# Summing modulation rows over the partitions: matmuls with a tile of ones, or transfers that accumulate in place

## The chip, the cores and the metric

The kernel runs on one core of a Trainium2 chip. The metric is the device time of one execution in microseconds (us); the median of three runs of the kernel before is 1470.62 us, from 1469.34 to 1471.14. A core has five engines with their own instruction queues, each run in order: TensorE (PE; its weight loads are shown as PEld), VectorE (DVE), ScalarE (ACT), GpSimd (POOL) and SyncE (SP). Here SP issues the loads of weights and the stores of the output, and POOL issues the small transfers of the modulation.

## The reference, cut to what matters

A layer of a diffusion backbone on 256 latent tokens and 256 context tokens of width 2048. A conditioning vector c gives six rows of 2048 numbers, by which the tokens are shifted, scaled and gated:

```python
mod = (jax.nn.silu(c) @ w_mod[l] + b_mod[l])[:, None, :]
sa, ca, ga, sm, cm, gm = jnp.split(mod, 6, axis=-1)
...
mix = token_mixer(q, k_all, v_all, p[..., P_OFF:G_OFF], p[..., G_OFF:], lam, lam_init, ...)
x = x + ga * mix
x = x + gm * sq_relu_mlp(modulate(x, norm_mlp_w[l], sm, cm), w_ff1[l], w_ff2[l])
```

`modulate(x, w, shift, scale)` is `rmsnorm(x, w) * (1 + scale) + shift`. The first two rows, `sa` and `ca`, are needed at the start. The four late ones, `ga`, `cm`, `sm` and `gm`, are needed from the output projection on. Each of them is a product of one vector of 2048 with a 2048 x 2048 matrix, plus a bias.

## The kernel before

All products of the layer are made of 128x512 or 128x256 tiles. A weight chunk of 128x1024 floats is loaded by SP into a `raw` tile (five buffers), ACT casts it to `whi` (L243), DVE subtracts to get the rest `wlo` (L244), three buffers each, and PE multiplies the high and the low part (`xstat`, L453, L454 and L459; `ff1`, L1061 and L1064). PE's instructions follow the order of the program, and so does most of DVE's; the rest is ordered by a scheduler when the kernel is built. The stages are: first modulation rows and the first q and k groups, then v, q, k, v groups, pooling (`pin`), gates (`pg`, `pyy`) beside attention, output projection (`wo`), and the MLP (`f`).

The four late rows are made beside this work, not on PE. `late_gen` (L612) is a generator that is advanced by one step whenever enough weight chunks have passed: a step loads one 128x1024 chunk of the row's matrix, and DVE multiplies it by 128 numbers of silu(c), one for each partition, and adds it to an accumulator (`late_part`, L651, tile `macc`). After 16 such steps the accumulator holds, for half a row (1024 columns), one partial sum in each of 128 partitions. Its start was a memset by POOL and a load of the bias into partition 0 (L632, L633). There are 4 rows of 2 halves.

The partial sums must be added over the partitions, and the sum is wanted in all 128 partitions, because it multiplies tokens, which lie in the partitions. That is done with PE: for each quarter row the 512 columns are split into a high and a low part (`late_half`: cast on ACT, L270, `ah`; subtraction on DVE, L271, `al`), and two matmuls with a 128x128 tile of ones (`late_sum`, L670 and L671) put the sum into every partition of a PSUM bank. ACT copies it to its place (L675), or, for `cm`, DVE adds 1 and multiplies by the norm weights (L673, tile `nmw`, loaded in 128 copies, L640). As `macc` has one buffer, what is left of a half is made up before the next begins (L627 to L630).

Where these steps stand in the queues is set by `later(n, fn)` (L96): it keeps a step back until n more weight chunks have been taken, and `tick` (L100) then writes it out. `pin` keeps an instruction in the written order on its engine.

The readers of the four rows: `ga_bc` in `projected` (L924), `cm` (first part of the tile `sb`) in `scaled` (L918), `sm` (second part of `sb`) in `shifted` (L955), `gm` at the end (L1092, L1104).

Other work on POOL near the change: sums of rotated q and k (`qraw`, L484), limits of squares in attention (`osq`, L754, read by PE's `osum`, L758), window sums of the pooling (`za`, L811 to L818), squares in the MLP (L1041, L1072).

Of the kernel before, what the change touches and what calls it, by code (L numbers as in the profile page):

```python
# [11 lines left out]
F32 = mybir.dt.float32  # L12
F32R = mybir.dt.float32r
AF = mybir.ActivationFunctionType
ALU = mybir.AluOpType
AX = mybir.AxisListType

P = 128
# [30 lines left out]
def layer(ctx: ExitStack, tc, a, out):  # L49
    nc = tc.nc  # L50
    pool = ctx.enter_context(tc.tile_pool(name="sb", bufs=1))
    psum = ctx.enter_context(tc.tile_pool(name="ps", bufs=8, space=bass.MemoryType.PSUM))
    pe, gp = nc.tensor, nc.gpsimd
    pin = tc.keep_in_program_order
    ordered = [False]
# [13 lines left out]
    act, vec, pe, sp = Engine(nc.scalar, ordered), Engine(nc.vector, ordered), Engine(nc.tensor, ordered_pe), nc.sync  # L69

    def bank(name):
        return psum.tile([P, 512], F32, tag="ps", name=name)

    def work(name, shape=None, dt=F32):
        return pool.tile(shape or [P, 512], dt, tag="w2", name=name, bufs=9)
# [14 lines left out]
    late = [None]  # L90
    credit = [0.0]
    credit_rate = [0.0]
# [3 lines left out]
    def later(n, fn):  # L96

        waiting.append([n, fn])
# [170 lines left out]
    def split(hi, lo, src):  # L269
        act.copy(hi, src)  # L270
        vec.tensor_sub(lo, src, hi.bitcast(F32))  # L271
# [33 lines left out]
        return prq[:, lo:hi]  # L305

    ident = pr("ident")
    ones = pool.tile([P, P], F32R, tag="ones", name="ones")
    vec.memset(ones.bitcast(F32), 1.0)
    ebias = pool.tile([P, 1], F32, tag="ebias", name="ebias")  # L310
    vec.memset(ebias, -32.0 * math.log(2.0))
    epsb = pool.tile([P, 1], F32, tag="epsb", name="epsb")
# [294 lines left out]


    ga_bc = s8("ga_bc", [P, D])
    parts = []  # L610

    def late_gen():  # L612
        for name in ("ga", "cm", "sm", "gm"):
            if name == "ga":
                dst = ga_bc
            elif name == "gm":
                mods["gm"] = None
                yield
                mods["gm"] = s8("gm_bc", [P, D])
                dst = mods["gm"]  # L620
            else:
                if "sb" not in mods:
                    mods["sb"] = s16("sb", [P, 2, D])
                dst = mods["sb"][:, 0 if name == "cm" else 1, :]
            for half in range(2):
                yield
                for part in parts:  # L627
                    if part in waiting:
                        waiting.remove(part)
                        part[1]()  # L630
                acc = pool.tile([P, 1024], F32, tag="macc", name="macc", bufs=1)
                gp.memset(acc, 0.0)  # L632
                nc.gpsimd.dma_start(acc[0:1, :], a["b_" + name][half])  # L633
                norm_w = []
                for k in range(KT):
                    raw = raw_chunk(a["w_" + name][half, k])
                    if name == "cm" and k == 8:
                        for q in range(2):
                            norm_w.append(work("nmw"))
                            nc.gpsimd.dma_start(norm_w[q], a["nmw"][2 * half + q])  # L640
                    later(2 if credit_rate[0] < 1 else 1, partial(late_part, acc, raw, k))
                    parts.append(waiting[-1])
                    if k == KT - 1:
                        o = dst[:, half * 1024:half * 1024 + 1024]
                        later(2 if credit_rate[0] < 1 else 1, partial(late_split, acc, norm_w, o))
                        parts.append(waiting[-1])
                    yield

    def late_part(acc, raw, k):

        pin(vec.scalar_tensor_tensor(acc, raw, sil[:, 0, k:k + 1], acc, ALU.mult, ALU.add))  # L651

    def late_split(acc, norm_w, o):
        for q in range(2):
            part = partial(late_half, q, acc, norm_w, o)
            if q == 0:
                part()
            else:
                later(2, part)
                parts.append(waiting[-1])  # L660

    def late_half(q, acc, norm_w, o):
        ah, al = work("ah", dt=F32R), work("al", dt=F32R)
        split(ah, al, acc[:, q * 512:q * 512 + 512])
        later(3, partial(late_sum, ah, al, norm_w[q] if norm_w else None, o[:, q * 512:q * 512 + 512]))

    def late_sum(ah, al, wr, o):

        ps = bank("late")
        pin(pe.matmul(ps, ones, ah, start=True, stop=False))  # L670
        pe.matmul(ps, ones, al, start=False, stop=True)  # L671
        if wr is not None:
            vec.scalar_tensor_tensor(o, ps, 1.0, wr, ALU.add, ALU.mult)  # L673
        else:
            act.copy(o, ps)  # L675

    late[0] = late_gen()

# [449 lines left out]
def _layout(inp):  # L1128
    f = {k: np.asarray(v) for k, v in inp.items()}
    m = {}  # L1130

    def put(name, arr):
        m[name] = np.ascontiguousarray(arr)

    for n, s in (("xT", "x"), ("cT", "ctx")):
        put(n, f[s][0].T.reshape(4, 4, P, T).transpose(0, 2, 1, 3))
    put("x", f["x"][0].reshape(2, P, 4, 512).transpose(0, 2, 1, 3))

    wm, bm = f["w_mod"][0], f["b_mod"][0]
    chunk = {n: slice(i * D, (i + 1) * D) for i, n in enumerate(("sa", "ca", "ga", "sm", "cm", "gm"))}  # L1140
    both = np.stack([wm[:, chunk[n]].reshape(4, 4, P, KT, 128) for n in ("ca", "sa")], 4)
    put("w_m", both.transpose(3, 0, 2, 1, 4, 5).reshape(KT, 4, P, 1024))
    for n in ("ga", "cm", "sm", "gm"):
        put("w_" + n, _ko(wm[:, chunk[n]]))
        put("b_" + n, bm[chunk[n]].reshape(2, 1, 1024))
    put("nmw", np.broadcast_to(f["norm_mlp_w"][0].reshape(4, 1, 512), (4, P, 512)))

    wi = f["w_in"][0]
    put("w_q", _xs(wi[:, 0:1024]))
    put("w_k", _xs(wi[:, 1024:2048]))  # L1150
    put("w_v", _xs(wi[:, 2048:3072]))
    put("w_p", _ws(wi[:, 3072:4096]))
    put("w_ga_in", _xs(wi[:, 4096:6144]))
    put("w_gb_in", _xs(wi[:, 6144:8192]))
    put("pool_w", f["pool_w"][0].reshape(4, 2, P, T).transpose(0, 2, 1, 3).reshape(4, P, 512))
    put("w_a", _xs(f["w_a_up"][0]))
    put("w_b", _xs(f["w_b_up"][0]))
    put("w_o", _xs(f["w_o"][0]))
    put("w_ff1a", _ko(f["w_ff1"][0][:, :1024])[0])
    put("w_ff1", _ws(f["w_ff1"][0][:, 1024:]))  # L1160
    w2 = f["w_ff2"][0].reshape(8, 1024, D)
    put("w_ff2", np.stack([_xs(w2[b]) for b in range(8)]))

    edge = []
    t = np.arange(T)
    for w in WINDOWS:
        cnt = np.clip(t + w // 2, 0, T) - np.clip(t - w // 2, 0, T)
        e = np.float32(w) / cnt.astype(np.float32)
        ee = np.concatenate([e[:w // 2], e[T - (w // 2 - 1):] if w > 2 else e[:0]])
        edge.append(np.concatenate([ee, np.zeros(2 * (w - 1) - len(ee), np.float32)]))  # L1170
    edge = np.concatenate(edge)
    pc = {"ident": np.eye(P, dtype=np.float32), "c": _cols(f["c"][0]), "cc": _cols(f["c_ctx"]),
          "bsa": _cols(bm[chunk["sa"]]), "bca": _cols(bm[chunk["ca"]]), "nw": _cols(f["norm_attn_w"][0]),
          "pscale": _cols(f["pool_scale"][0]), "subln": f["subln_w"][0][:, None],
          "edge": np.broadcast_to(edge, (P, len(edge))), "stack": np.tile(np.eye(32, dtype=np.float32), (4, 1))}
    prm = np.zeros((P, PRM_W), np.float32)
    for n, v in pc.items():
        lo = PRM[n][0]
        prm[:, lo:lo + v.shape[1]] = v
    m["prm"] = prm  # L1180

    inv = (np.float32(10000.0) ** (-np.arange(0, 32, 2, dtype=np.float32) / np.float32(32))).astype(np.float32)
    row = (t // 64).astype(np.float32)[:, None] * inv[None]
    col = (t % 64).astype(np.float32)[:, None] * inv[None]
    cos = np.concatenate([np.cos(row), np.cos(row), np.cos(col), np.cos(col)], 1)
    sin = np.concatenate([-np.sin(row), np.sin(row), -np.sin(col), np.sin(col)], 1)
    pc = {"cos": cos.reshape(2, P, 64).transpose(1, 0, 2).reshape(P, 128),
          "sin": sin.reshape(2, P, 64).transpose(1, 0, 2).reshape(P, 128),
          "wq": f["q_norm_w"], "wk": f["k_norm_w"], "lq1": f["lambda_q1"], "lk1": f["lambda_k1"],
          "lq2": f["lambda_q2"], "lk2": f["lambda_k2"]}  # L1190
    prq = np.zeros((P, PRQ_W), np.float32)
    for n, v in pc.items():
        lo, hi = PRQ[n]
        prq[:, lo:hi] = np.broadcast_to(v, (P, hi - lo))
    m["prq"] = prq
    return m
# [15 lines left out]
```

## Time and profile before

| | us |
|---|---|
| median of three runs | 1470.62 |
| the profiled execution | 1469.82 |
| its span, first to last instruction | 1467.8 |
| busy: PE / DVE / ACT / POOL | 1437.1 / 1000.2 / 683.5 / 121.3 |

How to read rows of the profile. In a timeline a row is: start in us, duration in us, engine, line, operation, tile written <- tiles read, shape, count, and in brackets how long the engine was idle before it and what ended that. Durations of matmuls overlap, so the pitch from start to start says what one costs. A row of a window is: stretch, its length, then for PE, PEld, DVE, ACT and POOL the busy time with the number of instructions, then the granted clock of PE as a share of full speed, the busy share of the DMA engines and GB/s. A row of a tile is: line, engine, operation, tile, count, shortest/median/longest duration in ns, first and last start; the row on landing gives the time from issue to the data's arrival of the transfers named above it.

### The profile page before, as it was taken

To read this page: it belongs to the slowest core of one execution; us is meant where nothing else is said; L and a number is where in the kernel's file an instruction comes from. 1 tells how busy PE (TensorE), PEld (TensorE's weight loads), DVE (VectorE), ACT (ScalarE), POOL (GpSimd) and SP (SyncE) were. 2 spreads that over 40 slices of the span, in tenths; PEclk is the share of its full clock that TensorE was granted. 3 is DMA by queue.
4 is the path that set the end of the run, shared out by engine and by line. 5 is a ranking of instruction groups with operands and counts; after the bars stand their busy time and mean duration, and the time that the engine had idled before them with its cause. 6 is when DMAs were issued, how large, how long until landed. Compare 5 with 4: busy or idle time off the path is not lost.

```text
span 1467.8 us, 19774 instructions
## 1 busy us (share of the span) xinstructions
PE 1437.1 (98%) x7466; PEld 1183.6 (81%) x7466; DVE 1000.2 (68%) x1243; ACT 683.5 (47%) x929; POOL 121.3 (8%) x120
## 2 busy tenths in 40 slices
PE   4999999999999999999999999999999999999998
PEld 3667887778878888888888888888888888888887
DVE  4667787868887786768676656666666655555675
ACT  4334336466554344435444554445344453544442
POOL 0001110101400000000001000001000000000260
PEclk8999999999999999999999999999999999999999
DMA  9996585435788888899646777767777655555554
GB/s 364 409 408 237 198 284 178 144 115 167 226 289 293 297 274 305 279 310 323 206 168 204 231 245 233 238 224 235 238 239 241 201 189 193 191 190 194 185 195 141
DMA packets 97439, 347.85 MB, mean 237 GB/s; under 512 B 11072, under 2 KB 11712, under 8 KB 97344
## 3 DMA queue, kind: packets, MB, share of 16 engines
q1 hardware_dynamic: 96768, 345.51, 69.6%
q8 instruction: 58, 0.95, 0.3%
q0 software_dynamic: 576, 1.08, 0.2%
q14 instruction: 37, 0.30, 0.1%
HBM read 344.45 MB, written 2.10 MB: 236 GB/s over the span
## 4 chain that ended last, share of the span: by engine, by line
PE 91%; DVE 4%; ACT 2%; DMA 1%; issue 1%; POOL 0%; DVEq 0%; SPq 0%; ACTq 0%; POOLq 0%
PE f L1061 14%; PE f L454 8%; PE f L453 8%; PE f L459 8%; PE f L1064 7%; PE pg L454 4%; PE pg L453 4%; PE pg L459 4%; PE w_k L67 3%; PE wo L453 2%; PE wo L454 2%; PE pyy L453 2%; PE pyy L459 2%; PE pyy L454 2%; PE wo L459 2%; PE v L459 2%
## 5 line engine op out<-in xcount | busy, mean ns | idle before, releaser
L244 DVE TENSOR_TENSOR wlo<-raw,whi 128x1024 fp32r<-128x1024 f32 (+1 forms) x430 | 534.7, 1245 | 341.6 <-ACT whi L243 319.6
L243 ACT CAST whi<-raw 128x1024 fp32r<-128x1024 f32 (+1 forms) x430 | 449.6, 1047 | 551.7 <-PE f L454 179.6
L1061 PE MATMUL f<-h,whi 128*128 128x512 f32 x896 | 224.3, 392 | 0.0
L454 PE MATMUL f<-whi,act 128*128 128x512 f32 x512 | 199.3, 389 | 0.0
L453 PE MATMUL f<-whi,act 128*128 128x512 f32 x512 | 199.3, 389 | 0.0
L1061 PEld LDWEIGHTS f<-h,whi 128*128 128x128 f32 x896 | 161.6, 189 | 29.2
L651 DVE SCALAR_TENSOR_TENSOR macc<-raw,sil,macc 128x1024 f32<-128x1024 f32 x128 | 165.0, 1289 | 4.0 <-issue 2.5
L459 PE MATMUL f<-wlo,act 128*128 128x512 f32 x512 | 136.8, 389 | 0.0
L1064 PEld LDWEIGHTS f<-h,wlo 128*128 128x128 f32 x896 | 122.2, 190 | 8.7
L1064 PE MATMUL f<-h,wlo 128*128 128x256 f32 x896 | 124.9, 282 | 0.0
L459 PEld LDWEIGHTS f<-wlo,act 128*128 128x128 f32 x512 | 96.1, 188 | 20.0
L454 PEld LDWEIGHTS f<-whi,act 128*128 128x128 f32 x512 | 96.1, 188 | 19.8
L453 PEld LDWEIGHTS f<-whi,act 128*128 128x128 f32 x512 | 96.1, 188 | 19.8
L453 PE MATMUL pg<-whi,hL 128*128 128x512 f32 x256 | 101.4, 396 | 0.0
L454 PE MATMUL pg<-whi,hL 128*128 128x512 f32 x256 | 100.6, 393 | 0.0
L1072 POOL TENSOR_TENSOR rsq<-relu 128x512 f32<-128x512 f32 x28 | 29.2, 1043 | 527.5 <-ACT relu L1071 497.0
L459 PE MATMUL pg<-wlo,hL 128*128 128x512 f32 x256 | 68.6, 390 | 0.0
L454 PEld LDWEIGHTS pg<-whi,hL 128*128 128x128 f32 x256 | 48.5, 189 | 10.3 <-issue 0.2
L453 PEld LDWEIGHTS pg<-whi,hL 128*128 128x128 f32 x256 | 48.5, 189 | 10.3 <-issue 0.2
L459 PEld LDWEIGHTS pg<-wlo,hL 128*128 128x128 f32 x256 | 48.4, 189 | 10.1
L632 POOL MEMSET macc<- 128x1024 f32 x8 | 7.6, 955 | 479.2 <-DVE al L271 374.9
L1086 DVE TENSOR_TENSOR acc<-f,acc 128x512 f32<-128x512 f32 x48 | 30.9, 686 | 19.6 <-PE f L459 19.6
(275 smaller groups left out, 2098.1 us busy)
## 6 DMA issues: line engine op xcount, KB each, us to landing
raw<-in_w_ff_dram SPq DMA_DIRECT2D x240, 512.0 KB, 4.2
raw<-in_w_m_dram SPq DMA_DIRECT2D x64, 512.0 KB, 9.8
raw<-in_w_ga_dram SPq DMA_DIRECT2D x32, 512.0 KB, 4.6
raw<-in_w_cm_dram SPq DMA_DIRECT2D x32, 512.0 KB, 4.6
raw<-in_w_gb_in_dram SPq DMA_DIRECT2D x32, 512.0 KB, 4.7
raw<-in_w_ga_in_dram SPq DMA_DIRECT2D x32, 512.0 KB, 5.0
raw<-in_w_sm_dram SPq DMA_DIRECT2D x32, 512.0 KB, 4.9
raw<-in_w_o_dram SPq DMA_DIRECT2D x32, 512.0 KB, 4.6
```

The source lines that it names most:

```text
L67: return (lambda *a, **k: pin(emit(*a, **k))) if self.flag[0] else emit
L243: act.copy(hi, raw)
L244: vec.tensor_sub(lo, raw, hi.bitcast(F32))
L453: pe.matmul(banks[t], tok(h, k, 0, tt), wt, start=k == 0, stop=False)
L454: pe.matmul(banks[t], tok(h, k, 1, tt), wt, start=False, stop=False)
L459: pe.matmul(banks[t], tok(h, k, 0, tt), wt, start=False, stop=k == 2 * nk - 1)
L632: gp.memset(acc, 0.0)
L651: pin(vec.scalar_tensor_tensor(acc, raw, sil[:, 0, k:k + 1], acc, ALU.mult, ALU.add))
L1061: pe.matmul(ps, hi[:, kk * P:kk * P + P], both(h2, k), start=k == 0, stop=False)
L1064: pe.matmul(ps[:, T:2 * T], lo[:, kk * P:kk * P + P], act_slice(h2, k, 0), start=False, stop=k == KT - 1)
L1072: gp.tensor_mul(sq, r, r)
L1086: vec.tensor_add(acc[:, t, gs], bs[t], acc[:, t, gs])
```

## The change

The accumulator tile `macc`, the split, the matmuls, the tile of ones and the copies go. The partial sums are now gathered in the place of the row itself (`o`, 1024 columns of `ga_bc`, `sb` or `gm_bc`), and added over the partitions by transfers: POOL issues a transfer of the upper 64 partitions onto the lower 64 that adds to what is there, then 32 onto 32, and so on to 1 onto 1: seven of them, each of which waits for the one before. Then partition 0 is stored to a scratch row in DRAM, and one more transfer reads that row into all 128 partitions. For `cm`, DVE first adds 1 and multiplies by the norm weights on partition 0 alone, for which 4 KB of weights per half are loaded instead of four times 256 KB. A fold is written out one weight chunk after the one before. The order of SP's loads is the same as before.

```diff
-                acc = pool.tile([P, 1024], F32, tag="macc", name="macc", bufs=1)
-                gp.memset(acc, 0.0)
-                nc.gpsimd.dma_start(acc[0:1, :], a["b_" + name][half])
+                o = dst[:, half * 1024:half * 1024 + 1024]
+                gp.memset(o, 0.0)
+                nc.gpsimd.dma_start(o[0:1, :], a["b_" + name][half])
...
-                        later(2 if credit_rate[0] < 1 else 1, partial(late_split, acc, norm_w, o))
-                        parts.append(waiting[-1])
+                        later(2 if credit_rate[0] < 1 else 1, partial(late_fold, o, norm_w, P // 2))
...
-    def late_sum(ah, al, wr, o):
-
-        ps = bank("late")
-        pin(pe.matmul(ps, ones, ah, start=True, stop=False))
-        pe.matmul(ps, ones, al, start=False, stop=True)
-        if wr is not None:
-            vec.scalar_tensor_tensor(o, ps, 1.0, wr, ALU.add, ALU.mult)
-        else:
-            act.copy(o, ps)
+    def late_fold(o, norm_w, n):
+
+        if n > 0:
+            nc.gpsimd.dma_start(o[0:n, :], o[n:2 * n, :], accum_op=ALU.add)
+            later(1, partial(late_fold, o, norm_w, n // 2))
+            return
+        if norm_w is not None:
+            vec.scalar_tensor_tensor(o[0:1, :], o[0:1, :], 1.0, norm_w, ALU.add, ALU.mult)
+        row = rows.tile([1, 1024], F32, tag="row", name="row")
+        nc.gpsimd.dma_start(row, o[0:1, :])
+        later(1, lambda: nc.gpsimd.dma_start(o, row.broadcast_to([P, 1024])))
```

The helpers that waited in `parts`, `late_split` and `late_half` go as well; `late_part` writes to `o` in place of `acc`.

On DVE, the place is the end of the first half of `cm`, in the gates. Before: the last sum into `macc`, then weight subtractions, the two subtractions `al` and, as their sums arrive from PE, the two products with `nmw`.

```order
L651 SCALAR_TENSOR_TENSOR macc<-raw,sil,macc 128x1024
L244 TENSOR_TENSOR wlo<-raw,whi 128x1024 x2
L271 TENSOR_TENSOR al<-macc,ah 128x512 x2
L244 TENSOR_TENSOR wlo<-raw,whi 128x1024
L673 SCALAR_TENSOR_TENSOR sb<-late,nmw 128x512
L244 TENSOR_TENSOR wlo<-raw,whi 128x1024
```

After the change the same last sum goes into `sb` (L641 now). Directly behind it stand these rows; the subtractions of weights are L245, the further L641 are products of the second half, and the product with `nmw` is L650.

```order
L245 TENSOR_TENSOR wlo<-raw,whi 128x1024 x4
L641 SCALAR_TENSOR_TENSOR sb<-raw,sil,sb 128x1024
L245 TENSOR_TENSOR wlo<-raw,whi 128x1024
L641 SCALAR_TENSOR_TENSOR sb<-raw,sil,sb 128x1024
L245 TENSOR_TENSOR wlo<-raw,whi 128x1024 x2
L641 SCALAR_TENSOR_TENSOR sb<-raw,sil,sb 128x1024
L245 TENSOR_TENSOR wlo<-raw,whi 128x1024 x2
L641 SCALAR_TENSOR_TENSOR sb<-raw,sil,sb 128x1024
L855 TENSOR_TENSOR sgm<-sgm,pyy_4141 128x512
L855 TENSOR_TENSOR sgm<-sgm,pyy_4142 128x512
L858 TENSOR_TENSOR sgm<-sgm 128x512 x2
L650 SCALAR_TENSOR_TENSOR sb<-sb,nmw 1x1024
```

The product with `nmw` has moved back: nine weight subtractions stand between it and the last sum of its half, and the next weight subtraction stands behind it.

On POOL, the place is the end of the second half of `ga`, where the pooling begins. Before, the second `osq` stands behind a memset, a load of the bias and four small memsets:

```order
L632 MEMSET macc 128x1024
L633 DMA macc<-in_b_cm_dram 1x16x64
L811 MEMSET za 128x8
L812 MEMSET za 128x8
L811 MEMSET za 128x8
L812 MEMSET za 128x8
L754 TENSOR_SCALAR osq<-osq 128x512
```

After the change the folds of 64, 32, 16, 8, 4 and 2 rows are issued ahead of it; each waits for the landing of the one before. (`osq` is L732 now, the folds are L646.) Behind the fold of 64 rows:

```order
L646 DMA ga_bc<-ga_bc 32x1024
L646 DMA ga_bc<-ga_bc 16x1024
L646 DMA ga_bc<-ga_bc 8x1024
L646 DMA ga_bc<-ga_bc 4x1024
L626 MEMSET sb 128x1024 x2
L627 DMA sb<-in_b_cm_dram 1x16x64
L789 MEMSET za 128x8
L790 MEMSET za 128x8
L789 MEMSET za 128x8
L790 MEMSET za 128x8
L646 DMA ga_bc<-ga_bc 2x1024
L732 TENSOR_SCALAR osq<-osq 128x512
```

The `osq` now waits for five landings that it did not wait for before.

More of the change, by code (lines that the diff above doesn't have):

```diff
@@ L52, in layer @@
     psum = ctx.enter_context(tc.tile_pool(name="ps", bufs=8, space=bass.MemoryType.PSUM))
+    rows = ctx.enter_context(tc.tile_pool(name="rows", bufs=2, space=bass.MemoryType.DRAM))
     pe, gp = nc.tensor, nc.gpsimd
@@ L307, in layer @@
     ident = pr("ident")
-    ones = pool.tile([P, P], F32R, tag="ones", name="ones")
-    vec.memset(ones.bitcast(F32), 1.0)
     ebias = pool.tile([P, 1], F32, tag="ebias", name="ebias")
@@ L609, in layer @@
     ga_bc = s8("ga_bc", [P, D])
-    parts = []
     def late_gen():
@@ L626, in late_gen @@
                 yield
[L627 to L630, printed above, removed]
-                acc = pool.tile([P, 1024], F32, tag="macc", name="macc", bufs=1)
-                gp.memset(acc, 0.0)
-                nc.gpsimd.dma_start(acc[0:1, :], a["b_" + name][half])
-                norm_w = []
+                o = dst[:, half * 1024:half * 1024 + 1024]
+                gp.memset(o, 0.0)
+                nc.gpsimd.dma_start(o[0:1, :], a["b_" + name][half])
+                norm_w = None
                 for k in range(KT):
@@ L637, in late_gen @@
                     if name == "cm" and k == 8:
[L638 to L641, printed above, removed]
-                    parts.append(waiting[-1])
+                        norm_w = pool.tile([P, 1024], F32, tag="macc", name="nmw", bufs=1)[0:1, :]
+                        nc.gpsimd.dma_start(norm_w, a["nmw"][half])
@@ L643, in late_gen @@
+                    later(2 if credit_rate[0] < 1 else 1, partial(late_part, o, raw, k))
                     if k == KT - 1:
-                        o = dst[:, half * 1024:half * 1024 + 1024]
-                        later(2 if credit_rate[0] < 1 else 1, partial(late_split, acc, norm_w, o))
-                        parts.append(waiting[-1])
+                        later(2 if credit_rate[0] < 1 else 1, partial(late_fold, o, norm_w, P // 2))
                     yield
-    def late_part(acc, raw, k):
-        pin(vec.scalar_tensor_tensor(acc, raw, sil[:, 0, k:k + 1], acc, ALU.mult, ALU.add))
@@ L653, in late_split @@
[L653 to L657, printed above, removed]
-            else:
[L659 to L665, printed above, removed]
@@ L667, in late_sum, with late_part @@
-    def late_sum(ah, al, wr, o):
-        ps = bank("late")
-        pin(pe.matmul(ps, ones, ah, start=True, stop=False))
-        pe.matmul(ps, ones, al, start=False, stop=True)
-        if wr is not None:
-            vec.scalar_tensor_tensor(o, ps, 1.0, wr, ALU.add, ALU.mult)
-        else:
-            act.copy(o, ps)
+    def late_part(o, raw, k):
+        pin(vec.scalar_tensor_tensor(o, raw, sil[:, 0, k:k + 1], o, ALU.mult, ALU.add))
+    def late_fold(o, norm_w, n):
[8 more added lines that the diff above has]
+        later(1, lambda: nc.gpsimd.dma_start(o, row.broadcast_to([P, 1024])))
@@ L1145, in _layout @@
         put("b_" + n, bm[chunk[n]].reshape(2, 1, 1024))
-    put("nmw", np.broadcast_to(f["norm_mlp_w"][0].reshape(4, 1, 512), (4, P, 512)))
+    put("nmw", f["norm_mlp_w"][0].reshape(2, 1, 1024))
     wi = f["w_in"][0]
```

## The prediction

> **What bounds the kernel now.** I read the page first, then TensorE's timeline, then VectorE's where the two meet.
>
> ```profile
> span 1467.8 us, 19774 instructions
> PE 1437.1 (98%) x7466; PEld 1183.6 (81%) x7466; DVE 1000.2 (68%) x1243; ACT 683.5 (47%) x929; POOL 121.3 (8%) x120
> PE 91%; DVE 4%; ACT 2%; DMA 1%; issue 1%; POOL 0%; DVEq 0%; SPq 0%; ACTq 0%; POOLq 0%
> ```
>
> TensorE (PE) is busy for 98% of the span and makes 91% of the chain that ended last. A matmul taken out of its queue is worth its pitch (the distance to the next start, not the overlapping 0.4 us of one), and a new wait of an idle engine is worth nothing until PE waits. POOL, which gets the new transfers, is busy for 8%. The 16 pairs of summing matmuls (L670, L671) stand in PE's timeline like this, first the undisturbed case, then the pair of the first half of `cm`:
>
> ```profile
> 446.21 0.40 PE L670 MATMUL late<-ah,ones 128*128 128x512 f32 x1
> 446.44 0.40 PE L671 MATMUL late<-al,ones 128*128 128x512 f32 x1
> 446.68 0.39 PE L453 MATMUL pg<-whi,hL 128*128 128x512 f32 x1
> ```
>
> ```profile
> 435.46 1.07 PE L459 MATMUL pg<-wlo,hL 128*128 128x512 f32 x4
> 437.29 0.49 PE L670 MATMUL late<-ah,ones 128*128 128x512 f32 x1 [0.76 <-ACT ah L270]
> 438.80 0.50 PE L671 MATMUL late<-al,ones 128*128 128x512 f32 x1 [1.01 <-DVE al L271]
> 439.13 0.47 PE L453 MATMUL pg<-whi,hL 128*128 128x512 f32 x1
> 439.40 0.63 PE L454 MATMUL pg<-whi,hL 128*128 128x512 f32 x1
> 439.82 0.63 PE L453 MATMUL pg<-whi,hL 128*128 128x512 f32 x1
> ...
> 443.48 0.39 PE L453 MATMUL pg<-whi,hL 128*128 128x512 f32 x1
> ```
>
> A pair costs 446.68 - 446.21 = 0.47 us of PE. At 437 the pair stands in PE's fixed order before its operands exist: PE waits for ACT, then for DVE, and afterwards matmuls start 0.42 us apart instead of 0.23. The windows show the granted clock there:
>
> ```profile
> 436.00:444.00 8.00, 6.23 (x20) 4.45 (x19) 5.35 (x7) 3.75 (x5) 2.55 (x4) 0.79 0.93 321
> 300.00:350.00 50.00, 50.00 (x316) 41.67 (x315) 35.34 (x54) 33.38 (x62) 5.38 (x11) 1.00 0.39 122
> 430.00:470.00 40.00, 38.23 (x164) 30.98 (x163) 31.89 (x32) 17.57 (x20) 2.55 (x4) 0.96 0.88 295
> 510.00:560.00 50.00, 50.00 (x226) 41.47 (x225) 37.88 (x38) 21.85 (x25) 1.47 (x2) 1.00 0.83 285
> ```
>
> The third last column is the clock: 0.79 over these 8 us. The one before last is the share of the DMA engines: 0.88 and 0.83 where `cm` is summed, 0.39 where `ga` is.
>
> **The change part by part.**
>
> *Removed from PE.* Fifteen pairs at 0.47 are 7.05 us. The pair of 437 costs more: four matmuls from 435.46 at 0.23 end their turn at 436.37, and the twelve matmuls from 439.13 need 2.73 at full pitch (443.48 to 446.21, one chunk) but end at 443.48. 443.48 - 436.37 - 2.73 = 4.38 us. What is late next there is nothing near: the `wlo` that the next chunk needs at 436.37 + 1.8 ends at 433.44 + 1.23 = 434.7 (first row below). Together 7.05 + 4.4 = 11.4 us, all on the path.
>
> *Removed from ACT and DVE.* Sixteen casts and subtractions, twelve copies and four products with `nmw`; no row shows PE waiting for them but the 437 one. I count nothing more. The memset of `ones` ends before anything waits for it: nothing.
>
> *Added.* In each of 8 halves POOL issues seven folds, a row store and a spread, each behind the landing of the one before. The trace has no accumulating transfer. The nearest rows are POOL's other transfers, the 4 KB biases (`macc`, over 200 to 350, then 430 to 620 us) and the 256 KB of `nmw`:
>
> ```profile
> L633 POOL DMA_DIRECT2D macc<-in_b_cm_dram x1: 568/568/568, 322.5 to 322.5; - x1
> DMA to landing us min/median/max: 1.9/2.0/2.2
> ```
>
> ```profile
> L633 POOL DMA_DIRECT2D macc<-in_b_sm_dram x2: 497/502/508, 524.6 to 603.5; - x2
> DMA to landing us min/median/max: 3.8/3.9/4.9
> ```
>
> ```profile
> L640 POOL DMA_DIRECT2D nmw<-in_nmw_dram x4: 538/584/644, 391.3 to 441.7; - x4
> DMA to landing us min/median/max: 3.1/4.9/6.4
> ```
>
> So issue to landing is 2.0 where the DMA engines are idle half the time and 3.8 to 4.9 where they are 0.83 to 0.88 busy, for 4 KB as for 256 KB. Ends for one fold: 1.9 and 6.4 us. I take 4.5 in the gates, between the medians 3.9 and 4.9, because these are rows of the same stretch; an accumulating transfer also reads its target, which nothing here prices.
>
> *Who waits for that.* For `ga`, `sm` and `gm` only late readers: nothing, as long as nine steps of 4.5, 41 us, are. SP's order of loads stays as it was, and what the new transfers add to its 0.83 to 0.88 share is small: a fold moves at most 256 KB, less than one 512 KB load, and 1 MB of `nmw` goes. For `cm` it is otherwise: the product with `nmw` (now one instruction on partition 0, which I price like the 1.28 of a 128x1024 product) stands in DVE's fixed order nine `wlo` subtractions behind the last product of its half, and waits there for all seven folds. Behind it on DVE stands the next `wlo`, and PE waits for that. DVE's rows of the first `cm` half, and PE's reading of that `wlo`:
>
> ```profile
> 433.44 1.23 DVE L244 TENSOR_TENSOR wlo<-raw,whi 128x1024 fp32r<-128x1024 f32 x1 [1.28 <-ACT whi L243]
> 434.59 1.28 DVE L651 SCALAR_TENSOR_TENSOR macc<-raw,sil,macc 128x1024 f32<-128x1024 f32 x1
> 435.78 2.36 DVE L244 TENSOR_TENSOR wlo<-raw,whi 128x1024 fp32r<-128x1024 f32 x2
> ...
> 461.47 1.29 DVE L880 TENSOR_TENSOR sgm<-sgm 128x512 f32<-128x512 f32 x2
> 462.68 1.22 DVE L244 TENSOR_TENSOR wlo<-raw,whi 128x1024 fp32r<-128x1024 f32 x1
> ```
>
> ```profile
> 471.16 0.61 PE L459 MATMUL pg<-wlo,hL 128*128 128x512 f32 x2
> ```
>
> The folds start at 434.59 + 1.28 = 435.9. DVE reaches the product at 462.7 - 4.4 = 458.3, since its turn is set by PE, which no longer loses 4.4. PE wants the `wlo` at 471.2 - 4.4 - 0.5 (one pair) = 466.3; with 1.28 + 1.22 of DVE in between the folds must have landed by 463.8, that is 27.9 us after their start, 4.0 us each. At 4.5 they land at 435.9 + 31.5 = 467.4: DVE stands for 9 us and PE for 3.6. While DVE stands it frees no `raw` tile, so loads stop and the last fold should come nearer to 2.0: PE then waits 1.1. I take 2.5.
>
> For the second half of `cm` the same with these rows:
>
> ```profile
> 515.92 1.28 DVE L651 SCALAR_TENSOR_TENSOR macc<-raw,sil,macc 128x1024 f32<-128x1024 f32 x1
> ...
> 541.66 1.23 DVE L244 TENSOR_TENSOR wlo<-raw,whi 128x1024 fp32r<-128x1024 f32 x1 [0.76 <-ACT whi L243]
> 544.18 1.23 DVE L244 TENSOR_TENSOR wlo<-raw,whi 128x1024 fp32r<-128x1024 f32 x1 [1.29 <-ACT whi L243]
> ```
>
> ```profile
> 551.89 0.62 PE L459 MATMUL pyy<-wlo,yb 128*128 128x512 f32 x2
> ```
>
> Start 517.2, wanted at 551.9 - 1.0 - 2.5 = 548.4: 31.2 us, or 4.45 a fold; without the 4.4 us by which the old stall let DVE run ahead of PE, up to 3 us less. At 4.5 PE waits 0.3 to 3; I take 1.5. Each such wait also costs the clock: by the rows at 437, 4.35 instead of 2.73 for twelve matmuls, 1.6 us, twice 3.2. Sum of what is added: 2.5 + 1.5 + 3.2 = 7.2 us.
>
> *POOL's own queue.* In the second half of `ga` five folds stand ahead of the second `osq` (row 328.45), whose PE reader has a fixed place:
>
> ```profile
> 307.56 1.28 DVE L651 SCALAR_TENSOR_TENSOR macc<-raw,sil,macc 128x1024 f32<-128x1024 f32 x1
> 328.45 1.49 POOL L754 TENSOR_SCALAR osq<-osq 128x512 f32<-128x512 f32 x1 [0.37 <-ACT osq L753]
> 339.50 1.02 PE L758 MATMUL osum<-osq,mean 128*128 128x512 f32 x2
> ```
>
> `osq` may start once the folds of 64 to 4 rows have landed, 308.8 + 5 x 2.0 = 318.8 in this quiet stretch, 331.3 at 4.5, and must start by 339.5 - 1.9 (four pairs) - 1.5 = 336.1. It costs nothing up to 5.4 us a fold: (336.1 - 308.8) / 5.
>
> *Sum:* 1469.82 (profiled execution: the span and 2.0 us around it) - 11.4 + 7.2 = 1465.6. That execution lies 0.8 us below the median of 1470.62, inside the runs' 1.8 us; against the median I say **1466**.
>
> **The rivals.**
>
> *Folds are cheap (A).* If a fold in the gates costs 2.2 us like the bias in the quiet stretch, seven end 15.4 us after their start, DVE never waits, and all 11.4 remain: 1458.4, said 1459. For it: size made no difference in the rows. Against it: the bias needed 3.8 to 4.9 exactly here. The Trainium skill (DMA: Bandwidth & Descriptors, section Anatomy of one DMA, SWDGE path) gives about 2.0 us fixed and the bytes at 436 GB/s, by which the seven folds would be an estimated 15.2 us and case A would hold; the 4.9 us of a 4 KB bias at 440 speaks against that figure here.
>
> *Folds are dear, slower than before (C).* The place is the `nmw` product in DVE's order. At 6.4 us a fold (the slowest `nmw` row) the seven take 44.8: PE waits 16.9 in the first half, 13.6 to 16.6 in the second, and 3.2 for the clock. That is some 35 lost against 11.4, so 1494. It decides from 4.7 us a fold on, where 7 x 4.7 - 27.9 + 7 x 4.7 - 29.8 + 3.2 is about 11.4. For it: the target is read too, nothing overlaps in the chain, and DVE is 76 to 80% busy there. Against it: only one transfer of POOL took that long. The Trainium skill (SBUF — State Buffer, section A bandwidth-pool intuition that's wrong) warns that VectorE in its two-port modes keeps GpSimd from writing descriptors; a transfer of about 0.6 us became about 3.1. By that each fold would gain some 2.5 us and case C would hold; the bias at 322.5 landed in 1.9 us with VectorE 71% busy, so the trace shows no such delay.
>
> *The time is not given back (D).* ACT waits for loads shortly before 436:
>
> ```profile
> 432.36 1.05 ACT L243 CAST whi<-raw 128x1024 fp32r<-128x1024 f32 x1 [2.65 <-DMA raw<-in_w_ga_in_dram]
> ```
>
> If PE only meets the next load instead of the 437 pair, 4.4 of the 11.4 are lost and the waits stay: 1469.8 + 0.2 = 1470. Against it: the next two `wlo` are done by 438.1 (the row of 435.78), before PE would want them.
>
> **How the numbers follow.** Forecast 0.33, A 0.22, C 0.33, D 0.12. A measurement of this kernel tells 0.2%, 2.9 us, from no change. Faster by more: A, two thirds of the forecast case and a little of D, 0.48. Slower by more: nearly all of C and the dear end of the forecast, 0.34. The rest is 0.18. The range reaches from A with the other waits of the pairs gone (1457) to C (1494). The forecast's own range is 1460 to 1473.
>
> **What would show it.** In the profile after: PE loses 32 matmuls, and between 436 and 444 the clock is 1.0. In POOL's rows seven folds of a `cm` half take about 31 us from first issue to the last landing; under 28 us means A, over 35 means C. The two `nmw` products on DVE show idle time before them, released by a DMA, 5 to 9 us for the first, and PE's wait on `wlo` right behind is 1 to 4 us with the clock halved after it. If `osum` waits for POOL, my quiet-stretch price is wrong. PE waiting elsewhere, for loads, would make it D.

## The result, and the profile after

| | median, us | ratio to before | 95% interval |
|---|---|---|---|
| the change | 1490.97 | 1.0131 | 1.0111 to 1.0151 |
| the change once more (e10) | 1489.16 | 1.0133 | 1.0118 to 1.0148 |

The kernel before took 1469.98 us beside the first and 1470.32 beside the second. One of the first four executions was disturbed, at 3236.05, and stands in that median but not in the ratio; the other three are 1485.48, 1488.72 and 1493.23. The profile is of the 1485.48 one. So the change is slower by 1.3%, clear of both intervals. The forecast was 1466, with a chance of 0.34 for slower.

First the page of the changed kernel: the span, the busy times, and the chain that ended last.

```profile
span 1483.7 us, 19761 instructions
PE 1435.9 (97%) x7434; PEld 1179.2 (79%) x7434; DVE 991.1 (67%) x1224; ACT 668.8 (45%) x901; POOL 170.1 (11%) x190
PE 71%; DMA 13%; DVE 8%; issue 4%; ACT 3%; POOL 1%; DVEq 0%; SPq 0%; ACTq 0%; POOLq 0%
```

PE has lost its 32 matmuls, and DMA now has 13% of the chain, where it had 1%: landings have come onto the path. What PE waited for from 430 to 700 us (total, times, longest):

```profile
PE pg L458 <- DVE wlo L245: 15.5, 3, 8.0
PE pyy L452 <- ACT whi L244: 1.9, 2, 1.5
PE pg L452 <- ACT whi L244: 0.7, 2, 0.4
```

The first line is what the prediction named: the `wlo` behind the product with `nmw`, in two long waits and one of 0.2. DVE's timeline around the two products, then PE's:

```profile
466.86 1.21 DVE L650 SCALAR_TENSOR_TENSOR sb<-sb,nmw 1x1024 f32<-1x1024 f32 x1 [6.32 <-DMA sb<-sb]
468.00 1.21 DVE L245 TENSOR_TENSOR wlo<-raw,whi 128x1024 fp32r<-128x1024 f32 x1
...
522.42 1.28 DVE L641 SCALAR_TENSOR_TENSOR sb<-raw,sil,sb 128x1024 f32<-128x1024 f32 x1
...
558.08 1.21 DVE L650 SCALAR_TENSOR_TENSOR sb<-sb,nmw 1x1024 f32<-1x1024 f32 x1 [10.10 <-DMA sb<-sb]
559.22 1.21 DVE L245 TENSOR_TENSOR wlo<-raw,whi 128x1024 fp32r<-128x1024 f32 x1
```

```profile
469.26 2.08 PE L458 MATMUL pg<-wlo,hL 128*128 128x512 f32 x4 [7.30 <-DVE wlo L245]
471.14 1.91 PE L871 MATMUL turnT<-prm,sgm 128*128 128x128 f32 x8
...
560.48 2.08 PE L458 MATMUL pg<-wlo,hL 128*128 128x512 f32 x4 [8.01 <-DVE wlo L245]
```

At 469.26 and 560.48 PE has stood for 7.30 and 8.01 us, and behind that four matmuls take 1.88 us (469.26 to 471.14) in place of 0.91. Matched one by one with the same matmuls before the change, PE loses another 2.1 and 2.5 us behind the two waits, until the pitch is full again. The windows at 437, where the stall was, and at these two places (the third last column is the clock, the one before last the share of the DMA engines):

```profile
436.00:444.00 8.00, 8.00 (x37) 6.64 (x36) 3.45 (x4) 1.76 (x3) 0.79 (x1) 1.00 1.00 306
461.00:474.00 13.00, 5.70 (x21) 4.51 (x20) 7.07 (x7) 2.24 (x4) 3.14 (x5) 0.74 0.34 114
552.00:567.00 15.00, 7.00 (x21) 5.26 (x20) 7.01 (x6) 1.61 (x2) 2.66 (x4) 0.66 0.34 101
```

From 436 to 444 PE is busy all the time at full clock: the stall of 437 is gone. While DVE stands the loads stop too: the share of the DMA engines is 0.34, and SP waits 10.5 us in the first stand for DVE's `wlo` before it issues the next load. The seven folds of the two `cm` halves take 32.6 us (434.17 to 466.73) and 34.0 us (523.99 to 557.99). Their sizes, from 430 to 650 us with the first half of `sm` (count, KB, median us from issue to landing):

```profile
sb<-sb POOLq DMA_DIRECT2D x3, 256.0 KB, 6.8
sb<-sb POOLq DMA_DIRECT2D x3, 128.0 KB, 6.1
...
sb<-sb POOLq DMA_DIRECT2D x3, 4.0 KB, 2.0
```

There is one more place, of which nothing in the prediction spoke: the last half of `gm` in the MLP. POOL, ACT and PE of the changed kernel:

```profile
1189.84 0.52 POOL L652 DMA_DIRECT2D row<-gm_bc  x1 [2.33 <-DMA gm_bc<-gm_bc]
1190.37 1.06 POOL L1050 TENSOR_TENSOR rsq<-relu 128x512 f32<-128x512 f32 x1
```

```profile
1191.46 0.62 ACT L271 CAST act<-rsq 128x512 fp32r<-128x512 f32 x1 [7.29 <-POOL rsq L1050]
```

```profile
1193.08 2.11 PE L1039 MATMUL f<-h,whi 128*128 128x512 f32 x8 [1.06 <-ACT whi L244]
```

The squares stand behind the folds on POOL, ACT stands for the squares, the next cast stands on ACT, and PE waits 1.06 us.

### The profile page after: what moved, and what is told of

Read it like the earlier page. It is cut to its first block, busy times and chain, and to the rows that moved or that the text cites. A ratio compares the mean times of both kernels' runs of the same rounds, so it can differ in the third digit from the quotient of the medians.

```text
span 1483.7 us, 19761 instructions
## 1 busy us (share of the span) xinstructions
PE 1435.9 (97%) x7434; PEld 1179.2 (79%) x7434; DVE 991.1 (67%) x1224; ACT 668.8 (45%) x901; POOL 170.1 (11%) x190
## 4 chain that ended last, share of the span: by engine, by line
PE 71%; DMA 13%; DVE 8%; issue 4%; ACT 3%; POOL 1%; DVEq 0%; SPq 0%; ACTq 0%; POOLq 0%
PE f L1039 13%; PE f L453 8%; PE f L452 8%; PE f L458 8%; PE f L1042 7%; PE w_k L68 3%; DMA raw<-in_w_ga_in_dram 3%; DVE wlo L245 3%; DMA sb<-sb 3%; DMA gm_bc<-gm_bc 2%; PE wo L452 2%; PE wo L458 2%; PE wo L453 2%; PE v L458 2%; PE v L453 2%
## 5 line engine op out<-in xcount | busy, mean ns | idle before, releaser
L245 DVE TENSOR_TENSOR wlo<-raw,whi 128x1024 fp32r<-128x1024 f32 (+1 forms) x430 | 535.3, 1248 | 345.1 <-ACT whi L244 319.5
L458 PEld LDWEIGHTS f<-wlo,act 128*128 128x128 f32 x512 | 96.1, 188 | 19.9
L641 DVE SCALAR_TENSOR_TENSOR sb<-raw,sil,sb 128x1024 f32<-128x1024 f32 x64 | 82.1, 1283 | 1.8 <-DMA sb<-in_b_cm_dram 1.8
L646 POOL DMA_DIRECT2D sb<-sb x28 | 22.2, 794 | 291.9 <-DVE sb L641 183.3
```

The source lines that it names most:

```text
L245: vec.tensor_sub(lo, raw, hi.bitcast(F32))
L458: pe.matmul(banks[t], tok(h, k, 0, tt), wt, start=False, stop=k == 2 * nk - 1)
L641: pin(vec.scalar_tensor_tensor(o, raw, sil[:, 0, k:k + 1], o, ALU.mult, ALU.add))
L646: nc.gpsimd.dma_start(o[0:n, :], o[n:2 * n, :], accum_op=ALU.add)
```

## The experiments

### Taking the stand away

**e1** is the changed kernel with the product further back; `pin` holds it in the written order.

```diff
-        if norm_w is not None:
-            vec.scalar_tensor_tensor(o[0:1, :], ...)
+        later(9 if norm_w is not None else 0, partial(late_row, o, norm_w))
+    def late_row(o, norm_w):
+        if norm_w is not None:
+            pin(vec.scalar_tensor_tensor(o[0:1, :], ...))
         row = rows.tile(...)
```

> The changed kernel with the product of cm and the norm weights kept back nine weight chunks and held in the written order on DVE: seven more weight subtractions stand ahead of it in each half. Folds, POOL's order up to the folds and SP's loads are the same. Theory (the loss is DVE standing at this product): the two waits of PE on wlo (7.3 and 8.0 us) and the half clock behind them (about 4.6 us) go, 1485.5 - 19.9 = about 1465, or 1462 if the load waits near 662 and 670 go too. Rival (the transfers themselves delay the loads of weights, and the product only shows it): PE meets the same waits elsewhere, for whi, and the time stays above 1478.

Measured 1473.43 (1466.7 to 1477.21), ratio 1.0022 (1.0008 to 1.0036): by the ratios about 16 us less than the change, but 8 more than the theory. PE's waits from 430 to 700 us:

```profile
PE pg L452 <- ACT whi L244: 2.7, 2, 2.4
PE pyy L452 <- ACT whi L244: 2.2, 4, 0.8
PE pg L458 <- DVE wlo L245: 1.1, 1, 1.1
```

The two stands are gone, and 6.0 us of other waits have come, 4.9 of them for `whi`. Before the longest, 2.4 us, ACT itself stood 7.42 us for a load of `raw`. So the loss was mostly the stand, as the theory says, and waits for loads came in place of a part of it, as the rival says.

**e7** is the changed kernel with the product on POOL instead, so that DVE waits for no fold.

```diff
-            vec.scalar_tensor_tensor(o[0:1, :], o[0:1, :], 1.0, norm_w, ALU.add, ALU.mult)
+            gp.tensor_scalar(o[0:1, :], o[0:1, :], 1.0, None, ALU.add)
+            gp.tensor_tensor(o[0:1, :], o[0:1, :], norm_w, ALU.mult)
```

> The changed kernel with the product of cm on POOL (an addition and a product on partition 0) in place of DVE; nothing is left out. DVE then waits for no fold. Theory (two losses: DVE's stand, about 17 us, and the folds' packets, about 7 us): like e1, 1472 to 1475. Rival (the stand alone counts): 1462 to 1465.

Measured 1475.22, ratio 1.0041 (1.0023 to 1.0059): within the two intervals the same as e1, by another way.

### What the removal is worth

**e2** is the kernel before without the sum over the partitions.

```diff
-        split(ah, al, acc[:, q * 512:q * 512 + 512])
-        later(3, partial(late_sum, ah, al, ...))
+        later(3, partial(late_copy, acc[:, q * 512:q * 512 + 512], ...))
```

> The kernel before without the sum over partitions: no split, no matmuls with ones, the accumulator is copied as it is (for cm multiplied by the norm weights). Leaves out the sum over the partitions. It prices what the change removes. Theory (the removal is worth what the sum said): 1469.8 - 7.5 (16 pairs at 0.47) - 4.4 (the stall at 437) = 1458. Rival (the stall is given back to the loads): 1462 to 1463.

Measured 1462.48, ratio 0.9951 (0.9936 to 0.9966), 7.65 below before. Its profile, matched matmul by matmul, is 2.69 us late at 34 us, ahead of all that the edit touches, and 7.32 early at the end. So 10.0 are won behind that point, 4.9 of it at 437 (the stall, and one pair), and none of it is given back in the gates. Whether the other executions of e2 began as late is not known: by their time alone the removal is worth 7.65.

**e3** is the kernel before with the matmuls of the sum later.

```diff
-        later(3, partial(late_sum, ah, al, ...))
+        later(5, partial(late_sum, ah, al, ...))
```

> The kernel before with the matmuls of the sum kept back five weight chunks after the split, not three. Nothing is left out. Theory: the stall at 437 goes and the 16 pairs stay: 1469.8 - 4.4 = 1465.4. Rival (the stall hid a wait for loads): 1469 to 1470.

Measured 1469.13, ratio 0.9996 (0.9983 to 1.0008). In its profile PE is 4.05 us ahead at 442 and 0.74 ahead at the end. From 430 to 700 us PE waits where it did not before:

```profile
PE pg L453 <- ACT whi L243: 0.6, 1, 0.6
PE pg L459 <- DVE wlo L244: 0.5, 1, 0.5
```

So with the split, the matmuls and the copies all still there, what the stall took is given back, 1.1 us of it in these two waits and the rest in pieces; with the split and the matmuls gone (e2) it stays won. Which of the removed pieces decides that, no run separates. The prediction's case D is right for e3 and wrong for e2.

### What a fold costs, and what it costs others

**e4** is the changed kernel with folds that only copy (`accum_op` left out).

> The changed kernel with folds that copy and do not add (same sizes, same chain); leaves out the sum over the partitions. Theory (a fold is dear because of issue, queue and landing in a loaded stretch): folds of cm stay at 4.6 to 4.9 us each, the waits of PE stay at 7 and 8 us, 1483 to 1490. Rival (adding to the target makes it dear): folds come down to about 3.9 us, the waits to 2 and 1.4 us, about 1472.

Measured 1482.86, ratio 1.0092 (1.0068 to 1.0116), on the theory's edge. Folds of `cm` take 4.43 and 4.51 us each, and PE waits 6.03 and 5.50. So adding to the target costs some 0.2 to 0.4 us of a fold, and most of a fold is the chain. The instruction that issues a fold on POOL is alone 0.27 us shorter here, 0.52 in place of 0.79. Adding is not free for the whole: e4 is 6 us faster than the change (e10), 3.8 of them in the two waits, and POOL's transfers take 4.0% of the engines' time from 430 to 650 us in place of 5.7%.

**e9** is the changed kernel with folds of 4 KB and the product at its old place in DVE's order: `dma_start(o[0:1, :], o[1:2, :], accum_op=ALU.add)` seven times.

> The changed kernel, product of cm on DVE at its place, with folds of one row each (4 KB); leaves out most of the sum over the partitions. The same without the stand (e5) took 1462.65. Theory (the stand is the length of the chain of seven landings, not their bytes): seven folds still take about 31 us, PE waits 6 to 8 us on wlo twice and the clock halves after each, 1462.65 + 15.3 + 4.6 = 1482, at least 1477. Rival (the stand came from the bytes of the folds): PE waits under 2 us, below 1468.

Measured 1473.86, ratio 1.0027 (1.0017 to 1.0037), between theory and rival. The seven folds take 28.0 and 28.9 us, 4.01 and 4.13 each. DVE and PE at the first product:

```profile
461.17 1.21 DVE L650 SCALAR_TENSOR_TENSOR sb<-sb,nmw 1x1024 f32<-1x1024 f32 x1 [4.80 <-DMA sb<-sb]
```

```profile
463.57 0.80 PE L458 MATMUL pg<-wlo,hL 128*128 128x512 f32 x1 [3.21 <-DVE wlo L245]
```

The second wait is 1.64 us. This is the run that tells where the deadline lies: at 4.01 us a fold PE waits 3.21, where the prediction has none up to 4.0. Per fold, 0.64 us more (4.65 in the changed kernel) should make that 7 x 0.64 = 4.5 more, 7.7; it was 7.30.

**e5** is e1 with folds of 4 KB.

> e1_product_later with folds that move one row each: seven transfers in the same chain and places, but 4 KB each instead of 256 to 4 KB; leaves out most of the sum over the partitions. Measured for e1: 1473.4, with load waits of PE of about 6 us between 440 and 660 and 1.6 us of half clock behind one. Theory (the folds' packets take time of DMA engines that the loads of the gates need): the waits shrink to 2 us or less, 1473.4 - 6 = 1467. Rival (the waits come from PE running 11 us ahead of what the loads can follow, or from buffers freed late, not from the folds' packets): 1472 to 1474. The price of one fold: if bytes make it dear, about 2 to 2.5 us in the gates; if issue and queue do, 4.5 us or more as in e1.

Measured 1462.65 (1462.36 to 1462.96), ratio 0.9956 (0.9941 to 0.997): 10.8 us less than e1 (9.7 by the ratios), more than expected. A fold still takes 4.72, 4.33 and 4.67 us in the gates; in e1 the same three halves take 5.67, 5.68 and 5.61. So the price of a fold is mostly that of any transfer in this stretch, and its bytes add 1.1 us. But the bytes are what the rest of the kernel pays for: matched matmul by matmul, e1 falls 7.7 us behind e5 between 430 and 690 us. The DMA queues from 430 to 650 us, of before, e1 and e5 (packets, MB, share of 16 engines; q0 is POOL's):

```profile
q1 hardware_dynamic: 17672, 63.82, 85.5%
q0 software_dynamic: 256, 0.54, 0.7%
```

```profile
q1 hardware_dynamic: 17410, 63.13, 83.7%
q0 software_dynamic: 1289, 2.66, 5.8%
```

```profile
q1 hardware_dynamic: 18104, 65.38, 86.2%
q0 software_dynamic: 1232, 1.68, 2.8%
...
sb<-sb POOLq DMA_DIRECT2D x21, 4.0 KB, 4.3
```

In e1 POOL's transfers hold 5.8% of the engines' time with 4% of the bytes, beside loads that hold 84%, and the loads move less in the same time than before the change; in e5 they move more. PE waits 1.8 us in e5's gates, 6.0 in e1's.

**e6** is e1 without the spread (the row goes to partition 0 alone).

> e1_product_later whose last transfer writes the row to partition 0 alone, not to all 128; leaves out the spread. Theory (DMA engine time): the spread has 28 of the about 75 engine microseconds of a half, so a third of the load waits goes, 1473.4 - 2.5 = about 1471. Rival (it is not the traffic): 1473.

Measured 1469.05 (1464.57 to 1473.21), ratio 0.9989 (0.9972 to 1.0007): 4.4 less than e1, in the direction of the theory and more than its 2.5. Its nine executions lie over 8.6 us, so the size is uncertain.

**e8** is the kernel before with `ga` and `gm` by folds, and `cm` and `sm` by matmuls as they were.

> cm and sm summed by matmuls as before the change, ga and gm by folds: no folds in the gates. Nothing is left out. Theory (folds harm only where the DMA engines are near full): no new load waits; 8 pairs less at 0.47 is 3.8 us, the waits behind POOL's queue (rows of q and k, squares of the MLP) cost 1.4 and 1.1: 1470.1 - 3.8 + 2.5 = 1468.8. Rival (folds harm everywhere): 1473 or more.

Measured 1470.3, ratio 1.0000 (0.9987 to 1.0013). There is no new load wait in the gates. Eight pairs are won, and in its profile they are lost again at 217, where PE waits 2.93 us on POOL, in a lower clock from 278 to 284 (1.5) and in the MLP; 2.6 come back from the stall of 437, which was shorter there, so that even this result is partly luck.

**e10** is the change once more (in the first table). **e11** is e1 once more, with no moved loads in spite of its label: 1471.04, a single execution.

> The changed kernel as it is, on the same chip as its variants. 1485 to 1493 as before.

> e1_product_later once more, on the same chip: 1467 to 1477 as before.

### POOL's queue, and the loads

The wait of e8's profile at 217 is in those of e1 and e11 too. First POOL's and PE's timelines of e1, then PE's of e11:

```profile
216.51 0.76 POOL L646 DMA_DIRECT2D ga_bc<-ga_bc  x1 [5.15 <-DMA ga_bc<-ga_bc]
217.03 1.60 POOL L483 TENSOR_TENSOR qraw<-qraw,qsq 128x512 f32<-128x512 f32 x1
```

```profile
218.69 0.65 PE L490 MATMUL qkT<-prm,qraw 128*128 128x128 f32 x4 [1.44 <-POOL qraw L483]
```

```profile
221.38 0.66 PE L490 MATMUL qkT<-prm,qraw 128*128 128x128 f32 x4 [3.21 <-POOL qraw L483]
```

The addition for the rotated q and k stands behind the third fold of `ga`, and PE's transposes wait for it. In the changed kernel's profile that was 0.36 us, in e10's 2.06.

**e12** is e1 with other rates of the late loads (`w_p` 0.5 to 1.0, the gates 0.6 to 0.5), so that fewer of them fall into the gates.

> e1_product_later with the loads of the late rows spread otherwise: a rate of 1.0 in place of 0.5 beside the pooling weights, 0.5 in place of 0.6 in the gates. Nothing is left out. Theory (the folds' packets harm because the DMA engines are near full in the gates): fewer loads there, so the load waits shrink from 6 us to 2 or 3: 1473.4 - 4 = 1469 to 1470. Rival (the share of the loads does not matter): 1473.

Measured 1470.31, ratio 1.0001 (0.9989 to 1.0013), close to the 1469 to 1470 expected. PE's waits from 200 to 700 us show why the gain is no larger: the gates are nearly free of waits (one of 0.3 us is not shown), and the pooling has longer ones (`pin`, `pd`).

```profile
PE pin L277 <- DVE wlo L245: 3.0, 2, 2.4
PE qkT L490 <- ACT e L706: 2.5, 1, 2.5
PE qkT L490 <- POOL qraw L483: 1.8, 1, 1.8
PE pd L277 <- DVE wlo L245: 1.1, 1, 1.1
```

**e13** is e1 with the addition of the rotated q and k on DVE.

```diff
-            gp.tensor_add(raw, raw, sq)
+            vec.tensor_add(raw, raw, sq)
```

> e1_product_later with the last addition of the rotated q and k on DVE, not on POOL, so that nothing on POOL that PE waits for in the k groups stands behind folds. Nothing is left out. Theory (one part of what is left of the loss is POOL's queue): the wait of PE at 217 to 221 (1.4 and 3.2 us in two profiles) and what follows it go: 1473.4 - 2.5 = 1471. Rival (all that is left are load waits in the gates): 1473.

Measured 1465.2, ratio 0.9977 (0.9962 to 0.9992), a larger gain than expected. **e14** has half of e12's shift of rates as well, and **e15** is the kernel before with both edits.

> e13 with half of the shift of loads of e12: rate 0.75 in place of 0.5 beside the pooling weights, 0.55 in place of 0.6 in the gates. Nothing is left out. Theory (two independent costs, POOL's queue and nearly full DMA engines in the gates): 1473.4 - 2.5 - 3 = 1468, which is under the kernel before. Rival: 1471 to 1473.

> The kernel before with the same two edits as e14 (addition on DVE, rates). Nothing is left out. Theory (both edits only mend what the folds cost): 1470, within 1.5 us of the kernel before. Rival (the edits help by themselves): 1467 or less, and then e14 says nothing of the folds.

Measured 1466.1, ratio 0.997 (0.9957 to 0.9982), and 1470.49, ratio 1.0000 (0.9992 to 1.0009). That looks like a changed kernel that beats the one before by its folds. It isn't: the profile of e13 had also lost a wait of the kernel before, shown here, and in e15 the rates had hidden that, since its profile falls back 8 us in the pooling.

```profile
277.39 0.63 PE L491 MATMUL qkT<-prm,qraw 128*128 128x128 f32 x4 [2.55 <-ACT e L724]
```

So **e16** is the kernel before with the addition on DVE alone, and **e17** is e13 on the same chip.

> The kernel before with the last addition of the rotated q and k on DVE: the control that e13 lacked. Nothing is left out. The profile of e13 has lost a wait of PE at 277 (2.55 us) that the kernel before has too. Theory: the edit is worth that wait and no more here, 1470.2 - 2.5 = 1467.7, so about 5.5 of the 8 us between e1 and e13 belong to POOL's queue behind the folds. Rival (the edit helps by itself as much as in e13): 1462 to 1464.

> e13 once more on the same chip as its control: 1465 median, 1464 to 1469.

Measured 1465.95, ratio 0.9971 (0.996 to 0.9982), and 1466.94, ratio 0.9981 (0.9969 to 0.9992). Both beat both kernels of the study, and do not differ from each other. The edit is worth 3.8 us without any fold. Of the 6.5 us from e1 to e17 (6.0 by the ratios) some 2 to 3 are left for POOL's queue. With the product later and the addition on DVE, folds and matmuls come out the same.

## Why the prediction was wrong

The mechanism was in it: the one place from which case C was to come, the product with `nmw` in DVE's order, is where the time went (e1, e7). The change was slower at a fold price at which I had it faster, because of these steps.

- *Removed, 11.4 us.* Right within 1.4 by e2's profile (10.0), within 3.8 by its time (7.65), and the clock is 1.00 from 436 to 444.
- *A fold at 4.5 us.* Near as a mean, 4.65 and 4.86 (in e10 4.61 and 4.72), but by luck. Issue to issue, the first five folds take 5.6 and 5.9 us each in the two halves, and the last two, while DVE stands, 2.3. That the last come down was foreseen; that the others are dearer was not. In e1, where DVE does not stand, the last two sizes are not cheap either, and a fold takes 5.6 to 5.7:

```profile
sb<-sb POOLq DMA_DIRECT2D x3, 8.0 KB, 4.5
sb<-sb POOLq DMA_DIRECT2D x3, 4.0 KB, 5.1
```

- *"PE wants the `wlo` at 471.2 - 4.4 - 0.5".* This is the step that failed. That row of PE reads the `wlo` of the next chunk. Numbering the subtractions and their readers, the `wlo` of 462.68 is read at 467.53, one chunk and the transposes earlier, and the one of the second half (544.18) at 549.17, not 551.89. The rows of before:

```profile
467.53 1.07 PE L459 MATMUL pg<-wlo,hL 128*128 128x512 f32 x4
...
549.17 1.07 PE L459 MATMUL pg<-wlo,hL 128*128 128x512 f32 x4
```

  With them the same sum gives 467.5 - 4.4 - 0.5 - 2.5 = 460.1, 24.2 us after the start or 3.5 a fold (in place of 4.0), and at 4.5 a wait of 467.4 - 460.1 = 7.3 us in place of 3.6, of which I took 2.5. Measured: 7.30. That this agrees to the last digit is luck: the seven folds took 1.1 us more than 31.5, but began 1.7 earlier, and PE came 0.7 earlier. e9 shows the deadline by itself. With this row the decision point of case C comes out at (24.2 + 28.5 + 11.4 - 3.2) / 14 = 4.35 us a fold, not 4.7: below the 4.5 that I took, so the same sum says slower. (28.5 is from the next point.) But only just, and by less than the runs can tell: 1469.8 - 11.4 + 7.3 + 3.0 + 3.2 = 1471.9. The row turns the sign; it is 6.3 of the 19.9 us between the sum's 1465.6 and the profiled 1485.48, and the rest is in the next points.
- *The second half, 1.5 us.* With the right row 545.7 - 517.2 = 28.5 us, or 3.0 us of wait at 4.5. It was 8.01: a fold took 4.86 (2.5 more), and DVE had lost lead, its last sum came at 522.42 in place of 515.92 while PE was 4.3 behind the time I had for it (2.2 more); 0.3 went by until the first issue. I had named up to 3 for that lead and taken little of it.
- *The clock, 1.6 each.* It was 2.1 and 2.5.
- *"What the new transfers add is small".* This is the second step that failed, a term put at nothing. With the stand gone, folds of full size cost 10.8 us against folds of 4 KB (e1, e5), some 2 to 3 of it through POOL's queue and about 1 through the MLP's squares; 7.7 are lost between 430 and 690 us, where PE waits for loads. I counted bytes, not time on the engines.
- *For `ga` and `gm` "only late readers: nothing".* Wrong by who stands behind them on POOL: q and k at 217 (0.36 to 3.21 us in eight profiles with full folds, 0.2 in that of e6, none in e5 and e9 with folds of 4 KB) and the squares at 1190 (1.06). The one reader that I priced, `osum`, did not wait, although a fold of that half took 3.7 us and not the 2.0 of the quiet stretch.

In the profile, matched matmul by matmul: two waits 15.3 and their clock 4.6, the squares 1.2 and q and k 0.4, and a further 5.9 between 440 and 690, 2.6 of it as single waits for `whi`, against 11.4 removed. That makes 16.0, and the span grew by 15.9.

How the folds' packets delay the loads is not settled. The engines' share is 0.90 in e1 and 0.89 in e5 from 430 to 650 us, and the loads' landing times in the same lists differ by no more than 0.4 us; that the share decides was argued, not shown. What is shown is that the cost goes with the bytes of the folds (e5) and, less surely, of the spread (e6), and leaves the gates when loads do (e12).

## What to carry to other kernels

When a wait moves into an in-order queue, the deadline is set by the reader of the next thing behind it: find that reader by numbering writes and reads, not by looking for a plausible row, since one chunk here turned 7.3 us into 3.6. The chain of small transfers cost its count of landings at the price that the stretch had for them, and its bytes cost the loads in the gates, where the share of the DMA engines was 0.90. A price that was measured beside a stand is not the price without it. And an edit that mends the new kernel must be tried on the old one alone: e13 looked like a win of the folds until e16.

## What the runs showed of the hardware

A 4 KB transfer of POOL lands in 2.0 us with the DMA engines at 0.34, and in 4.3 at 0.89. The Trainium skill (DMA: Bandwidth & Descriptors, section Anatomy of one DMA, SWDGE path) has about 2.0 us plus the bytes; the first agrees, and in the gates of the changed kernel seven folds of 4 KB to 256 KB took 32.6 to 40.4 us where that gives an estimated 15.2.

That DVE's work holds such transfers up was a rival in the prediction's case C. In e5's profile the price goes with the share of the DMA engines while DVE is about as busy: seven 4 KB folds landed in 2.2 us (median) from 310 to 334 us, with DVE busy for 66% and a share of 0.35, and in 3.7 from 947 to 975, with DVE at 63% and a share of 0.74. What the share itself does to a landing, no run takes apart.

A stand of PE does not always cost the clock. The wait of 2.5 us before `qkT` is followed by full clock in the kernel before and by a clock of 0.66 in e2 (windows of the 5 us behind it):

```profile
278.00:283.00 5.00, 5.00 (x24) 3.86 (x24) 1.29 (x5) 2.56 (x4) 0.00 (x0) 1.00 0.70 251
```

```profile
279.00:284.00 5.00, 4.80 (x17) 4.04 (x18) 2.02 (x4) 2.40 (x6) 0.00 (x0) 0.66 0.77 287
```
